# Softmax divisions ahead of the gated outputs, an output projection by tiles, and weight sums at period ends, in a one-core encoder kernel

## The chip, the cores and the metric

The kernel runs on one core of a Trainium2 chip. The metric is the device time of one execution in microseconds (us); smaller is better. The core has five engines that work side by side, each through its own queue in order: TensorE (PE, matmuls; its weight loads are shown apart as PEld), VectorE (DVE), ScalarE (ACT), GpSimd (POOL) and SyncE (SP, which issues DMAs).

## The reference

Two inputs, a prompt of 2048 tokens and a sample of 512, each of width 1024, go through the same two layers and a final RMSNorm. All is float32.

```python
# layer 0: windowed grouped-query attention, 16 heads of 64, 4 key/value heads
h = rmsnorm(x, g)
z = h @ w_in                                  # q, k, v, gate
scores = q . k * 64**-0.5 + bias              # |i-j| <= 128: blocks of 128 queries see 3 blocks of keys
m = max(max(scores), sink)
p = exp(scores - m)
p = p / (sum(p) + exp(sink - m))              # the division of this case
o = p @ v
x = x + (o * silu(gate)) @ w_out              # gated outputs, output projection
# layer 1: h = rmsnorm(x); f = Re(2-D DFT of h, per channel group)
x = x + (f * silu(h @ w_gate)) @ w_fout
y = rmsnorm(x, final_norm)
```

## The kernel before

Every large float32 product is made of three matmuls in a faster format: each operand is split into a high part and a low part (the rest), and hi·hi, hi·lo and lo·hi are summed (`matmul3`, L95). So most tiles exist as a high part, cast by ScalarE, and a low part, subtracted by VectorE or GpSimd.

**Stages.** The attention layer goes over five chunks of 512 tokens: chunk 0 is the sample, 1 to 4 the prompt. The Fourier layer follows. A chunk begins with h, k and v, and then has 17 *periods*, n = 0 to 16. Period n takes two blocks of 128 queries (b0 and b1) of one pair of heads (j = 0, 1; pair p = n // 2) through the first half of attention, and the two blocks of the period before ("old") through the second half:

- first half: `scores` (PE, L441, into three banks `spt`), `biased` (DVE, L460: adds the bias, finds the row's extreme), `exps` (ACT, L468, with the row's sum), `divide` (a reciprocal on DVE, L476, then a multiplication of the block by it: on ACT, L478, or on DVE, L480; in chunk 0 the form on DVE that also writes its accumulator, L484);
- second half, in the next period: `transp` (PE, L499: four banks `pt`), `parts` (hi by ACT, L507; lo by DVE, L508), `av` (PE, L525), `out_evac` (t2, a copy by ACT, L534; two sums o by DVE, L543, which free the bank; o times the gate on POOL, L545), and, one period later, `split` of the gated output uT (hi by ACT, L548; lo by POOL, L549).

PE's time between these is filled with pieces (`work`) of the next pair's q and gate projections, 8 pieces of three matmuls each, with `quota` saying how many pieces stand in each half of a period. When a projection is complete, its evacuation follows: `evac_q` (ACT L388, DVE L389, in chunk 0 after a scaling at L284) or `evac_g` (ACT L396, DVE L398). In the last periods there is no such work left, and pieces of the output projection (`op`, L95) take its place: uT times the weights wo, half of the 1024 columns at a time, four tiles of 128 tokens, in the three `spt` banks and one of five rotating banks; what remains of it (`tail`) is done before the next chunk's k and v.

**Extras** are steps for later stages, put at fixed quarters of a period: squares of the next chunk's tokens (ACT, L162), parts of sums of the Fourier layer's weights (`gate_sums`, `out_sums`: copies by ACT, L643 and L680, pieces by POOL, L624) and their stores. `AT` is the list of quarters of the weight sums.

**Order.** Each engine executes its queue in order. `seq` ties an instruction behind the one that was last tied on the same engine, and `after` ties it behind a named one; everything that is not tied a scheduler may move. A head pair's `start` loads its bias rows and copies two columns into them (DVE, L422 and L423). Times in the text are from the profiled execution, and a "+" in front of one counts from the start of a period's first scores.

Of the kernel before, what the change touches and what calls it, by code (L numbers as in the profile page):

```python
# [43 lines left out]
def encoder(  # L44
# [97 lines left out]
    def attention_phase():  # L142

        with ExitStack() as es:
# [265 lines left out]
            def attention(c, p, res, uTs):  # L410
# [61 lines left out]
                def divide(b, j):  # L472
# [3 lines left out]
                    seq(DVE, DVE.reciprocal(den, den))  # L476
                    if j:
                        seq(ACT, ACT.activation(s[:, ks], s[:, ks], AF.Copy, scale=den))  # L478
                    elif c:
                        seq(DVE, DVE.tensor_scalar(s[:, ks], s[:, ks], den, None, ALU.mult))  # L480
                    else:


                        seq(DVE, DVE.tensor_scalar(s[:, ks], s[:, ks], den, None, ALU.mult, ALU.add, accum_out=s[:, 386:387]))  # L484
# [74 lines left out]
            def out_proj(c, uTs):  # L559
# [3 lines left out]

                def mm(half, k):
                    if k == 0:

                        st["ps"] = (spt if half == 0 else []) + [bank(f"op{c}_{half}_{i}") for i in range(3 * (1 - half), 4)]
                    if k % 2 == 0:
                        st["w"] = load_w(c, 20 + half * 4 + k // 2, f"o{c}_{half}_{k}")
                    hi, lo = st["w"]  # L570
                    ws = slice((k % 2) * 512, (k % 2) * 512 + 512)
                    for i in range(4):
                        cs = slice(i * P, (i + 1) * P)
                        a = (uTs[k][0][:, cs], uTs[k][1][:, cs])
                        matmul3(st["ps"][i], a, (hi[:, ws], lo[:, ws]), k == 0, k == KD - 1)
# [34 lines left out]

                for half in range(2):
                    for k in range(KD):
                        steps.append(lambda half=half, k=k: mm(half, k))
                    steps.append(lambda half=half: evac(half))
                return steps
# [10 lines left out]
            def gate_sums(k):  # L626
# [10 lines left out]
                def lower():  # L637
                    b21 = rows[1][:, 0]
                    t = xtile([P, 2, 512], F32R, f"wB21_{k}")
                    after(ACT.copy(t[:, 0], b21), last_exp[0])  # L640
                    pieces(t[:, 1], b21, f32(t[:, 0]), ALU.subtract)
# [15 lines left out]
            def out_sums(k):  # L657
# [19 lines left out]
                def split(dst, row, half):  # L677
                    src = rows[row][:, half]
                    t = xtile([P, 2, 512], F32R, f"e{k}_{row}{half}")
                    after(ACT.copy(t[:, 0], src), last_exp[0])  # L680
                    pieces(t[:, 1], src, f32(t[:, 0]), ALU.subtract)
# [13 lines left out]
            stores = []  # L695
            AT = (1, 2, 5, 9, 11, 15, 16, 19, 23, 27, 28, 31, 32)
            EXTRA = {c: dict(zip(AT, gate_sums(c - 1) + out_sums(c - 1))) for c in range(1, 5)}
            for steps in EXTRA.values():
                steps.update({i: store for i in (4, 12, 18, 30, 34)})

# [41 lines left out]
            for c in range(len(CHUNKS)):  # L742
# [31 lines left out]
                m = 15 * KD - ahead_n  # L774
                quota = [m * (i + 1) // 27 - m * i // 27 for i in range(27)] + [3, 3, 2]
                assert sum(quota) == len(work) - ahead_n
# [20 lines left out]
                for n in range(17):  # L797
# [13 lines left out]
                    if new:  # L811
                        for j in range(2):
                            new[0].biased(new[1], j)
                        new[0].scores(new[1] + 1, (spt[2], spt[0]))
                    if old:
                        for b in range(2):
                            old[0].parts(old[1] + b)
                    if new:
                        for j in range(2):
                            new[0].exps(new[1], j)  # L820
                        for j in range(2):
                            new[0].biased(new[1] + 1, j)
                    for i in range(quota[2 * n] if n < 15 else 0):
                        work.pop(0)()
                    if n >= 15:
                        for i in range(n - 14):
                            op.pop(0)()
                    if new:
                        new[0].divide(new[1], 0)
                        for j in range(2):  # L830
                            new[0].exps(new[1] + 1, j)
                    if split:
                        split()
                        split = None
                    for i in range(4 * n, 4 * n + 2):
                        extra(i)
                    if old:
                        old[0].av(old[1])
                    if new:
                        new[0].divide(new[1], 1)  # L840
                        new[0].divide(new[1] + 1, 0)
                    if old:
                        split = old[0].out_evac(old[1])
                    if new:
                        new[0].divide(new[1] + 1, 1)
                    for i in range(4 * n + 2, 4 * n + 4):
                        extra(i)
                    if n < 15:
                        for i in range(quota[2 * n + 1]):
                            work.pop(0)()  # L850
                    elif n == 15:
                        op.pop(0)()
                    else:
                        split()
                        for i in range(3):
                            op.pop(0)()
                chain.pop(PE)
# [808 lines left out]
```

## Time and profile before

| what | value |
|---|---|
| time, three runs | 1708.18, 1713.01, 1712.97 us (median 1712.97) |
| profiled execution | 1707.01 us, span 1705.2 us, mean granted clock 0.983 |
| busy share of the span | PE 96%, PEld 79%, DVE 65%, ACT 54%, POOL 26% |
| attention layer's periods, chunks 0 to 4 | from about 42 us to 1128 us of the span |
| q1 (SP's DMA queue) | 81708 packets, 297.91 MB, 50.3% of 16 engines' span |

The span is the time from the first to the last instruction of the profiled execution; its own time, 1707.01 us, is 1.8 us more. "Busy" counts an engine's instructions, not its waits. PEclk or granted clock is the share of TensorE's full speed that the chip's throttle allowed. An arrow "<-" behind an instruction names what ended the engine's idle time before it. L numbers are lines of the kernel before.

### The profile page before, as it was taken

Reading aid. Unit: us, or ns where it says so; the run is one execution under the profiler, and the core shown is the slowest. Engines: PE = TensorE matmul, PEld = TensorE weight load, DVE = VectorE, ACT = ScalarE, POOL = GpSimd, SP = SyncE. Lnnn points to the kernel's source line nnn. Section 1 sums busy time; section 2 is a strip of 40 time slices with the busy share of each in tenths; the row PEclk is TensorE's granted clock in tenths of the full one; section 3 lists DMA queues with packets and bytes.
Section 4 is the critical chain, followed back from the end, with each engine's and each line's share of the span. In section 5 each row is a group of like instructions: output and inputs, shape, how many; then the busy total and the mean of one; then the engine's idle time right before and its main releaser. Section 6 shows DMA issues by size and latency. Waiting matters only on the chain.

```text
span 1705.2 us, 27749 instructions
## 1 busy us (share of the span) xinstructions
PE 1632.8 (96%) x9835; PEld 1348.5 (79%) x9835; DVE 1104.6 (65%) x2703; ACT 918.6 (54%) x2123; POOL 437.5 (26%) x605
## 2 busy tenths in 40 slices
PE   9888899999999998999999999989999999999998
PEld 7676688777797776887777877778888888888886
DVE  5766645676536665447764266656776667989686
ACT  6666633777516776247783176654545554443342
POOL 2344461332312421404223033121211111101010
PEclk9988999999999999999999999999999999999999
DMA  7467586756575564756556765566644568745862
GB/s 293 176 219 262 172 276 254 241 188 235 183 253 205 185 224 158 279 207 229 179 184 231 261 241 180 185 228 229 246 162 173 190 240 324 268 187 196 316 218 99
DMA packets 100646, 374.17 MB, mean 219 GB/s; under 512 B 12140, under 2 KB 22380, under 8 KB 83101
## 3 DMA queue, kind: packets, MB, share of 16 engines
q1 hardware_dynamic: 81708, 297.91, 50.3%
q0 software_dynamic: 16464, 70.30, 10.6%
q10 hardware_dynamic: 2336, 4.20, 0.7%
q8 instruction: 78, 1.28, 0.3%
q14 instruction: 60, 0.48, 0.1%
HBM read 281.10 MB, written 91.26 MB: 218 GB/s over the span
## 4 chain that ended last, share of the span: by engine, by line
PE 68%; ACT 9%; DVE 8%; DMA 8%; issue 4%; POOL 2%; SPq 0%; DVEq 0%; POOLq 0%; ACTq 0%
PE spt L95 8%; PE op L95 8%; PE qp L95 8%; PE gp L95 7%; PE fo L95 6%; PE W L95 6%; PE vp L95 3%; PE z L95 3%; PE spt L441 3%; ACT S L478 3%; PE Z L95 3%; PE Wo L95 2%; PE av L525 2%; DVE o L543 2%; PE pt L499 2%
## 5 line engine op out<-in xcount | busy, mean ns | idle before, releaser
L95 PE MATMUL gp<-h,wg 128*128 128x512 f32 x960 | 244.4, 403 | 0.0
L95 PE MATMUL qp<-h,wq 128*128 128x512 f32 x960 | 241.0, 401 | 0.0
L95 PEld LDWEIGHTS gp<-h,wg 128*128 128x128 f32 x960 | 178.4, 192 | 45.1 <-issue 10.3
L95 PEld LDWEIGHTS qp<-h,wq 128*128 128x128 f32 x960 | 178.2, 191 | 42.4 <-issue 5.2
L468 ACT ACTIVATE S<-S 128x385 f32<-128x385 f32 (+1 forms) x320 | 189.3, 602 | 22.5 <-DVE S L460 22.5
L508 DVE TENSOR_TENSOR pts<-pt,pts 128x384 fp32r<-128x384 f32 (+1 forms) x320 | 148.4, 523 | 41.0 <-ACT pts L507 40.8
L460 DVE CUSTOM_DVE_ANT_0 S<-spt,b 128x385 f32<-128x385 f32 (+1 forms) x320 | 156.1, 525 | 27.4 <-PE spt L441 26.9
L478 ACT ACTIVATE S<-S 128x384 f32<-128x384 f32 (+1 forms) x160 | 95.0, 595 | 102.8 <-DVE S L476 101.3
L549 POOL TENSOR_TENSOR uT<-o,uT 128x256 fp32r<-128x256 f32 x75 | 61.8, 823 | 328.2 <-ACT uT L548 328.1
L95 PE MATMUL op<-wo,uT 128*128 128x512 f32 x600 | 142.6, 389 | 0.0
L441 PE MATMUL spt<-kwin,qab 64*128 64x384 f32 (+1 forms) x960 | 129.4, 362 | 13.0 <-DVE S L460 9.9
L95 PE MATMUL fo<-wo,tTu 128*128 128x512 f32 x576 | 138.9, 392 | 0.0
L95 PEld LDWEIGHTS op<-wo,uT 128*128 128x128 f32 x600 | 112.7, 188 | 23.6
L507 ACT CAST pts<-pt 128x384 fp32r<-128x384 f32 (+1 forms) x320 | 124.4, 472 | 12.2 <-PE pt L499 10.3
L543 DVE TENSOR_TENSOR o<-av,t 64x256 f32<-64x256 f32 x150 | 62.6, 417 | 102.2 <-ACT t L534 94.3
L499 PE MATMUL pt<-ident,S 64*128 64x64 f32 x1792 | 89.4, 228 | 34.9 <-ACT S L478 19.5
L95 PEld LDWEIGHTS fo<-wo,tTu 128*128 128x128 f32 x576 | 106.0, 188 | 20.2
L525 PE MATMUL av<-pts,v 128*128 128x512 f32 (+1 forms) x576 | 118.7, 345 | 2.5 <-ACT pts L507 1.9
L525 PEld LDWEIGHTS av<-pts,v 128*128 128x128 f32 x576 | 101.0, 189 | 24.7 <-ACT pts L507 3.9
L441 PEld LDWEIGHTS spt<-kwin,qab 64*128 64x128 f32 x960 | 81.1, 189 | 45.1 <-issue 19.4
L499 PEld LDWEIGHTS pt<-ident,S 64*128 64x128 f32 x1792 | 76.9, 138 | 50.1 <-ACT S L478 29.2
L95 PE MATMUL spt<-wo,uT 128*128 128x512 f32 x360 | 97.4, 419 | 10.8 <-DVE S L460 10.8
(304 smaller groups left out, 2947.2 us busy)
## 6 DMA issues: line engine op xcount, KB each, us to landing
wo<-wsd SPq DMA_DIRECT2D x32, 1024.0 KB, 5.8
wq<-wsd SPq DMA_DIRECT2D x31, 1024.0 KB, 6.5
wg<-wsd SPq DMA_DIRECT2D x31, 1024.0 KB, 4.8
x<-x1d SPq DMA_DIRECT2D x40, 512.0 KB, 3.7
b<-b21d SPq DMA_DIRECT2D x40, 512.0 KB, 5.7
b<-rowd SPq DMA_DIRECT2D x40, 384.0 KB, 4.4
xs<-in_x_dram SPq DMA_DIRECT2D x23, 512.0 KB, 6.5
s2d<-gt POOLq DMA_DIRECT2D x40, 256.0 KB, 3.6
```

The source lines that it names most:

```text
L95: pe(PE.matmul(out, a[i], b[j], start=start and i + j == 0, stop=stop and i == 1, skip_group_check=more))
L441: pe(PE.matmul(banks[j][:, 2 + k0 * P : 2 + k1 * P], res["q"][rows, qp, b * P : (b + 1) * P], kwin[g][rows, kp, b * P + k0 * P : b * P + k ...
L460: seq(DVE, DVE.tensor_tensor_reduce(out=s[:, e0:e1], in0=ps[:, 1 + e0 : 1 + e1], in1=st["bias"][:, j, 386 - e1 : 386 - e0][:, ::-1], scale ...
L468: last_exp[0] = seq(ACT, ACT.activation(s[:, e0:e1], s[:, e0:e1], AF.Exp, bias=s[:, 386:387], scale=-1.0, accum_out=s[:, 387:388]))
L478: seq(ACT, ACT.activation(s[:, ks], s[:, ks], AF.Copy, scale=den))
L499: pe(PE.transpose(ps[h][:, kb, j, :], ss[j][rows, 1 + kb * P : 1 + (kb + 1) * P], ident[rows, rows]))
L507: seq(ACT, ACT.copy(hi, ps[:, k0:k1]))
L508: seq(DVE, DVE.tensor_tensor(lo, ps[:, k0:k1], f32(hi), ALU.subtract))
L525: pe(PE.matmul(to, v, pt, start=n == part == 0, stop=part == 1 and n in (1, len(todo) - 1), skip_group_check=n > 1,))
L543: seq(DVE, DVE.tensor_tensor(o[64 * j : 64 * j + 64], ps[0:64, :, j], t2[:, :, j], ALU.add))
L549: low = eng.tensor_tensor(lo, o, f32(hi), ALU.subtract)
```

## The change

Four things are edited. (1) In `divide`, one of four multiplications in a period stays on ScalarE (block b0, j = 1); the other three are on VectorE, where two were. (2) In a period, block b1's biased scores and exponentials and all four divisions are now issued ahead of the first half's projection pieces, av and `out_evac`; in period 15 both blocks' biased scores come ahead of `parts`. (3) All extras of a period stand at its end, `AT` and the stores' quarters are shifted, and ScalarE's copies of the weight sums are tied in its chain. (4) The output projection is issued by tiles: tile 3, in its bank, for k = 0 to 5, then tiles 0 to 2 for k = 0 to 5, then all tiles; its first four pieces stand in period 14. Periods 14, 15 and 16 hold 24, 33 and 39 matmuls of projections (before 15, 24 and 60), period 13 holds 24 (before 21).

```diff
-                    if j:
+                    if j > b % 2:
                         seq(ACT, ACT.activation(s[:, ks], s[:, ks], AF.Copy, scale=den))
                     elif c:
                         seq(DVE, DVE.tensor_scalar(s[:, ks], s[:, ks], den, None, ALU.mult))
...
-                def mm(half, k):
-                    if k == 0:
+                def mm(half, k, tiles):
+                    if k == 0 and 3 in tiles:
                         st["ps"] = (spt if half == 0 else []) + [bank(f"op{c}_{half}_{i}") for i in range(3 * (1 - half), 4)]
-                    if k % 2 == 0:
-                        st["w"] = load_w(c, 20 + half * 4 + k // 2, f"o{c}_{half}_{k}")
-                    hi, lo = st["w"]
+                    if k % 2 == 0 and 3 in tiles:
+                        st["w", k // 2] = load_w(c, 20 + half * 4 + k // 2, f"o{c}_{half}_{k}")
+                    hi, lo = st["w", k // 2]
...
-                    for i in range(4):
+                    for i in tiles:
...
-                for half in range(2):
-                    for k in range(KD):
-                        steps.append(lambda half=half, k=k: mm(half, k))
-                    steps.append(lambda half=half: evac(half))
+                steps += [lambda k=k: mm(0, k, (3,)) for k in range(6)]
+                steps += [lambda k=k: mm(0, k, range(3)) for k in range(6)]
+                steps += [lambda k=k: mm(0, k, range(4)) for k in range(6, KD)]
+                steps.append(lambda: evac(0))
+                steps += [lambda k=k: mm(1, k, range(4)) for k in range(KD)]
+                steps.append(lambda: evac(1))
...
-                    after(ACT.copy(t[:, 0], b21), last_exp[0])
+                    seq(ACT, ACT.copy(t[:, 0], b21))
...
-                    after(ACT.copy(t[:, 0], src), last_exp[0])
+                    seq(ACT, ACT.copy(t[:, 0], src))
...
-            AT = (1, 2, 5, 9, 11, 15, 16, 19, 23, 27, 28, 31, 32)
+            AT = (1, 4, 6, 9, 13, 17, 18, 20, 23, 26, 27, 32, 33)
...
-                steps.update({i: store for i in (4, 12, 18, 30, 34)})
+                steps.update({i: store for i in (7, 12, 22, 30, 37)})
...
-                quota = [m * (i + 1) // 27 - m * i // 27 for i in range(27)] + [3, 3, 2]
+                quota = [m * (i + 1) // 27 - m * i // 27 for i in range(27)] + [4, 4]
...
+                    if n == 15:
+                        for j in range(2):
+                            new[0].biased(new[1] + 1, j)
                     if old:
                         for b in range(2):
                             old[0].parts(old[1] + b)
                     if new:
                         for j in range(2):
                             new[0].exps(new[1], j)
-                        for j in range(2):
-                            new[0].biased(new[1] + 1, j)
-                    for i in range(quota[2 * n] if n < 15 else 0):
-                        work.pop(0)()
-                    if n >= 15:
-                        for i in range(n - 14):
-                            op.pop(0)()
-                    if new:
+                        if n < 15:
+                            for j in range(2):
+                                new[0].biased(new[1] + 1, j)
                         new[0].divide(new[1], 0)
                         for j in range(2):
                             new[0].exps(new[1] + 1, j)
+                        new[0].divide(new[1], 1)
+                        for j in range(2):
+                            new[0].divide(new[1] + 1, j)
+                    for i in range(quota[2 * n] if n < 15 else 18 - n):
+                        (work or op).pop(0)()
                     if split:
                         split()
                         split = None
-                    for i in range(4 * n, 4 * n + 2):
-                        extra(i)
                     if old:
                         old[0].av(old[1])
-                    if new:
-                        new[0].divide(new[1], 1)
-                        new[0].divide(new[1] + 1, 0)
-                    if old:
                         split = old[0].out_evac(old[1])
-                    if new:
-                        new[0].divide(new[1] + 1, 1)
-                    for i in range(4 * n + 2, 4 * n + 4):
+                    for i in range(4 * n, 4 * n + 4):
                         extra(i)
-                    if n < 15:
-                        for i in range(quota[2 * n + 1]):
-                            work.pop(0)()
-                    elif n == 15:
-                        op.pop(0)()
-                    else:
+                    if n == 16:
                         split()
-                        for i in range(3):
-                            op.pop(0)()
+                    half = quota[2 * n + 1] if n < 14 else 4 if n == 14 else 2
+                    for i in range(half):
+                        (work or op).pop(0)()
```

How the engines' queues change is shown at three places. Names carry chunk, pair, block and j: S2_5_0_1 is chunk 2, pair 5, block 0, j = 1; o, t2, av and pts name the old blocks' tiles; th and qab are the evacuations of a gate and of q; xs are the next chunk's tokens.

ScalarE in period 10 of chunk 2, before:

```order
L507 CAST pts2_4_2_6841<-pt2_4_3_1_6857 128x6x64
L468 ACTIVATE S2_5_0_0_6870<-S2_5_0_0_6870 128x385
L468 ACTIVATE S2_5_0_1_6872<-S2_5_0_1_6872 128x385
L396 ACTIVATE th2_5_6906<-gp2_5_6817 128x512
L468 ACTIVATE S2_5_1_0_6890<-S2_5_1_0_6890 128x385
L468 ACTIVATE S2_5_1_1_6892<-S2_5_1_1_6892 128x385
L548 CAST uT2_4_6335<-o2_4_0_6809 128x256
L162 ACTIVATE xs3_0_6815,ss3_6417<-xs3_0_6815 128x1024
L478 ACTIVATE S2_5_0_1_6872<-S2_5_0_1_6872 128x384
L534 COPY t22_4_2_6932<-av2_4_2_6919 64x512
L478 ACTIVATE S2_5_1_1_6892<-S2_5_1_1_6892 128x384
L507 CAST pts2_5_0_6966<-pt2_5_0_0_6967 128x6x64
```

and after:

```order
L507 CAST pts2_4_2_6841<-pt2_4_3_1_6857 128x6x64
L468 ACTIVATE S2_5_0_0_6870<-S2_5_0_0_6870 128x385
L468 ACTIVATE S2_5_0_1_6872<-S2_5_0_1_6872 128x385
L468 ACTIVATE S2_5_1_0_6890<-S2_5_1_0_6890 128x385
L468 ACTIVATE S2_5_1_1_6892<-S2_5_1_1_6892 128x385
L162 ACTIVATE xs3_0_6815,ss3_6438<-xs3_0_6815 128x1024
L478 ACTIVATE S2_5_0_1_6872<-S2_5_0_1_6872 128x384
L396 ACTIVATE th2_5_6916<-gp2_5_6817 128x512
L548 CAST uT2_4_6335<-o2_4_0_6809 128x256
L534 COPY t22_4_2_6931<-av2_4_2_6922 64x512
L162 ACTIVATE xs3_1_6938,ss3_6438<-xs3_1_6938 128x1024
L507 CAST pts2_5_0_6966<-pt2_5_0_0_6967 128x6x64
```

One division (L478) is left, ahead of the gate's evacuation (L396) and of t2 (L534); a square (L162) stands between t2 and the next period's casts (L507).

VectorE in the same period, before:

```order
L398 SCALAR_TENSOR_TENSOR s2_5_6908<-th2_5_6906,gp2_5_6817 128x512
L476 RECIPROCAL S2_5_0_0_6870<-S2_5_0_0_6870 128x1
L480 TENSOR_SCALAR S2_5_0_0_6870<-S2_5_0_0_6870 128x384
L476 RECIPROCAL S2_5_0_1_6872<-S2_5_0_1_6872 128x1
L476 RECIPROCAL S2_5_1_0_6890<-S2_5_1_0_6890 128x1
L480 TENSOR_SCALAR S2_5_1_0_6890<-S2_5_1_0_6890 128x384
L543 TENSOR_TENSOR o2_4_2_6934<-av2_4_2_6919,t22_4_2_6932 64x256 x2
L476 RECIPROCAL S2_5_1_1_6892<-S2_5_1_1_6892 128x1
L460 ISA S2_5_2_0_6995<-spt0_227,b2_5_6584 128x385
```

and after:

```order
L476 RECIPROCAL S2_5_0_0_6870<-S2_5_0_0_6870 128x1
L294 CAST kwin_230<-kwin_230 128x2x256
L480 TENSOR_SCALAR S2_5_0_0_6870<-S2_5_0_0_6870 128x384
L476 RECIPROCAL S2_5_0_1_6872<-S2_5_0_1_6872 128x1
L476 RECIPROCAL S2_5_1_0_6890<-S2_5_1_0_6890 128x1
L480 TENSOR_SCALAR S2_5_1_0_6890<-S2_5_1_0_6890 128x384
L476 RECIPROCAL S2_5_1_1_6892<-S2_5_1_1_6892 128x1
L480 TENSOR_SCALAR S2_5_1_1_6892<-S2_5_1_1_6892 128x384
L398 SCALAR_TENSOR_TENSOR s2_5_6918<-th2_5_6916,gp2_5_6817 128x512
L543 TENSOR_TENSOR o2_4_2_6933<-av2_4_2_6922,t22_4_2_6931 64x256 x2
L460 ISA S2_5_2_0_6995<-spt0_227,b2_5_6580 128x385
```

A third multiplication (L480) has come, and the last reciprocal no longer stands behind the sums o (L543); the gate's evacuation (L398) now stands behind the divisions. In chunk 0, where q is scaled first, the copy of two bias columns stands in this group after the change:

```order
L476 RECIPROCAL S0_1_2_1_920<-S0_1_2_1_920 128x1
L422 COPY b0_3_993<-sk_295 128x2
L423 COPY b0_3_993<-sk_295 128x2
L476 RECIPROCAL S0_1_3_0_938<-S0_1_3_0_938 128x1
L484 TENSOR_SCALAR S0_1_3_0_938<-S0_1_3_0_938 128x256
L476 RECIPROCAL S0_1_3_1_940<-S0_1_3_1_940 128x1
L484 TENSOR_SCALAR S0_1_3_1_940<-S0_1_3_1_940 128x256
L389 SCALAR_TENSOR_TENSOR qab0_2_956<-qp0_2_823,qab0_2_956 128x512
```

Before, L422 stood between the scaling of q (L284) and L389, ahead of all four divisions of the period; now L389 stands behind them.

TensorE in period 15 of chunk 2, before (the end of block b1's scores, then pieces of the projection):

```order
L441 MATMUL spt0_227<-kwin_230,qab2_7_7275 128x384
L95 MATMUL spt0_227<-wo2_0_0_7490,uT2_0_5586 128x512 x3
L95 MATMUL spt1_228<-wo2_0_0_7490,uT2_0_5586 128x512 x3
L95 MATMUL spt2_229<-wo2_0_0_7490,uT2_0_5586 128x512 x3
L95 MATMUL op2_0_3_7489<-wo2_0_0_7490,uT2_0_5586 128x512 x3
L525 MATMUL av2_7_0_7510<-pts2_7_0_7436,v1_4_3050 128x512 x2
```

and after:

```order
L441 MATMUL spt0_227<-kwin_230,qab2_7_7285 128x384
L95 MATMUL op2_0_3_7430<-wo2_0_4_7516,uT2_4_6335 128x512 x3
L95 MATMUL op2_0_3_7430<-wo2_0_4_7516,uT2_5_6584 128x512 x3
L95 MATMUL spt0_227<-wo2_0_0_7431,uT2_0_5586 128x512 x3
L95 MATMUL spt1_228<-wo2_0_0_7431,uT2_0_5586 128x512 x3
L95 MATMUL spt2_229<-wo2_0_0_7431,uT2_0_5586 128x512 x3
L525 MATMUL av2_7_0_7535<-pts2_7_0_7453,v1_4_3050 128x512 x2
```

Six matmuls of tile 3, in its own bank, now stand between the last scores and the first use of the score banks by the projection.

## The prediction

> **What bounds the kernel.** I read the page's engine shares first, then TensorE's waits, then windows by stage, then the timeline around one wait.
>
> ```profile
> span 1705.2 us, 27749 instructions
> ...
> PE 1632.8 (96%) x9835; PEld 1348.5 (79%) x9835; DVE 1104.6 (65%) x2703; ACT 918.6 (54%) x2123; POOL 437.5 (26%) x605
> ```
>
> TensorE (PE) is the bound: it idles only 1705.2 − 1632.8 = 72.4 us. The change adds no matmul and takes none away, so all it can win is this idle time and what the clock loses after it. TensorE's waits, longest sums first (total us, times, longest):
>
> ```profile
> PE pt L499 <- ACT S L478: 19.5, 52, 0.5
> PE pt L499 <- DVE o L543: 12.8, 16, 1.2
> PE spt L95 <- DVE S L460: 10.8, 5, 2.4
> PE spt L441 <- DVE S L460: 9.9, 10, 2.0
> PE spt L441 <- DVE qab L389: 3.1, 3, 1.7
> ```
>
> All five end at instructions that the change moves: the division on ScalarE (L478), the sums o that free a bank (L543), the biased scores (L460) and the low part of q (L389). They make 56.1 us. The third has five cases, one for each chunk.
>
> Windows by stage follow (start:end, length, then busy us and count for PE, PEld, DVE, ACT, POOL, then the granted clock). Rows 1, 3, 5, 7, 9 are periods 0 to 14 of the five chunks, rows 2, 4, 6, 8, 10 are period 15 up to the end of av. The last four are single periods: one without a wait and one with a stall in chunk 0, then the same for the prompt chunks.
>
> ```profile
> 42.20:201.50 159.30, 140.55 (x886) 108.72 (x885) 112.40 (x365) 109.54 (x274) 73.83 (x107) 0.93 0.59 209
> 201.50:213.10 11.60, 7.75 (x51) 6.20 (x51) 6.85 (x26) 6.61 (x17) 4.79 (x7) 0.85 0.53 173
> 292.80:432.90 140.10, 133.63 (x940) 106.32 (x939) 93.91 (x325) 101.53 (x265) 42.85 (x57) 1.00 0.61 207
> 432.90:445.00 12.10, 8.23 (x51) 6.39 (x51) 6.23 (x23) 5.87 (x16) 1.45 (x2) 0.86 0.56 184
> 519.70:664.30 144.60, 137.70 (x982) 109.44 (x981) 98.39 (x324) 105.53 (x265) 43.28 (x57) 1.00 0.58 200
> 664.30:677.20 12.90, 9.19 (x58) 7.12 (x58) 6.61 (x23) 6.04 (x16) 1.46 (x2) 0.74 0.51 173
> 751.80:893.30 141.50, 137.01 (x981) 109.20 (x980) 98.31 (x325) 104.36 (x262) 43.15 (x57) 1.00 0.57 199
> 893.30:906.00 12.70, 9.16 (x57) 7.15 (x57) 6.56 (x23) 6.04 (x16) 1.46 (x2) 0.73 0.52 177
> 974.70:1115.80 141.10, 135.52 (x937) 108.36 (x936) 95.18 (x318) 96.48 (x253) 41.83 (x57) 0.98 0.55 197
> 1115.80:1128.00 12.20, 8.15 (x57) 6.54 (x57) 6.07 (x21) 5.83 (x16) 1.47 (x2) 0.86 0.84 302
> 92.80:101.60 8.80, 8.80 (x65) 7.16 (x64) 7.30 (x14) 7.45 (x18) 7.38 (x12) 1.00 0.43 120
> 77.40:92.80 15.40, 12.21 (x65) 9.06 (x64) 10.76 (x37) 7.65 (x20) 6.15 (x10) 0.78 0.76 270
> 616.30:625.50 9.20, 9.20 (x69) 7.49 (x68) 6.23 (x21) 7.43 (x19) 1.68 (x2) 1.00 0.59 229
> 1019.00:1031.80 12.80, 11.15 (x71) 8.77 (x70) 7.90 (x26) 7.98 (x20) 7.78 (x11) 0.87 0.55 201
> ```
>
> First reading: idle is length less PE busy, 18.8, 6.5, 6.9, 4.5 and 5.6 us in the periods, 3.9, 3.9, 3.7, 3.5 and 4.1 at the ends: 61.4 of the 72.4. Second: a stall costs more than its idle time. The same 65 matmuls took 8.80 us and 15.40: 6.60 lost, 3.19 of it idle, the rest under a clock of 0.78. In the last pair 3.6 were lost, 1.65 idle. So about 2 us go for each idle us of a long stall.
>
> [...]
>
> **The pool to win.** I held the 14 periods 1 to 14 of each chunk against a no-wait period of their shape (8.80 to 9.2 us, less 0.24 for each matmul that a late period lacks); the excess sums to 32.3 us in chunk 0 and 7.9, 10.4, 7.3 and 8.5 in the others, 34.1 together. An end has 12 matmuls fewer than a full period, 9.20 − 12 × 0.24 = 6.3 us (5.9 for the two of x51): excess 5.7, 6.2, 6.6, 6.4, 5.9 = 30.8. All: 97.2 us. The profiled execution took 1707.01 us, its span and 1.8 beside it, 0.35% under the median of 1712.97; the floor is 1707.0 − 97.2 = 1609.8.
>
> **Divisions and order in the period.** One chain of chunk 2:
>
> ```profile
> 625.16 0.58 ACT L534 COPY t<-av 64x512 f32<-64x512 f32 x1
> ...
> 625.84 0.85 DVE L543 TENSOR_TENSOR o<-av,t 64x256 f32<-64x256 f32 x2 [1.85 <-ACT t L534]
> ...
> 626.98 0.62 ACT L478 ACTIVATE S<-S 128x384 f32<-128x384 f32 x1 [1.24 <-DVE S L476]
> ...
> 627.65 0.40 PE L499 MATMUL pt<-ident,S 64*128 64x64 f32 x6 [0.44 <-ACT S L478]
> ```
>
> The period's last division stands behind t2 and o, and the next period's transposes wait for it, 0.44 us here. After, all four divisions stand ahead of av. From the order and durations I schedule a period from its first scores: exponentials end at +5.6 us (block 1's scores are biased by +4.7), divisions at +7.0, t2 at +7.8, o at +8.7; the next transposes start at 9.2 + 0.7 = +9.9. So the first two waits have over 1 us of slack. ScalarE loses 80 × 0.62 us, one a period: 7.43 to 6.8 of 9.20. VectorE gains one of these (minimum/median/maximum ns):
>
> ```profile
> L480 DVE TENSOR_SCALAR S<-S x128: 349/423/834, 299.2 to 1123.0; 128x384 f32<-128x384 f32 x112, 128x256 f32<-128x256 f32 x16
> L484 DVE TENSOR_SCALAR_CACHE_REDUCE S<-S x32: 480/545/616, 46.8 to 208.7; 128x256 f32<-128x256 f32 x16, 128x384 f32<-128x384 f32 x16
> ```
>
> 64 of 0.42 in the prompt chunks, 16 of 0.55 with a short read in chunk 0: 6.23 to 6.7 of 9.20, so 2.5 us stay free, and I cost the 80 at nothing. If that cover went, they would cost 80 × 0.42 = 34. Prompt chunks: 34.1 falls to about 10, a gain of 24 (bounds: 5, below).
>
> **Chunk 0** is another matter:
>
> ```profile
> 74.20 2.82 POOL L119 TENSOR_TENSOR wq<-w32q,wq 128x256 fp32r<-128x256 f32 x4
> ...
> 74.65 3.55 DVE L422 COPY b<-sk 128x2 f32<-128x2 f32 x1
> ```
>
> The seven such copies of the chunk, grouped:
>
> ```profile
> L422 DVE COPY b<-sk 128x2 f32<-128x2 f32 x7 | 12.0, 1709 | 0.1
> ```
>
> A copy of 2 columns (L422) takes 3.55 us while POOL computes a weight's low parts, and everything on VectorE queues behind it. The stalled period of 15.40 follows directly. Three so held make 11.3 of the 12.0 us. Each precedes a stalled period (15.4, 14.2 and 15.8 us against 8.8): 19 of the 32.3. After, the copy stands among block 1's divisions, where POOL can hold it just as well; behind it now wait two divisions (1.4 us) and then q's low part (L389), which the next scores need. I take it that two of three recur at some 5 us and that the remaining 13 falls to 6: 16 stay, a gain of 16. Bounds: 4 left if none meets a string; 19 + 3 × 2 × 1.4 + 4 = 31 left if all do.
>
> [...]
>
> **Extras at the period's end.** Squares and copies for later weights now stand behind t2, and the next casts of p (L507) must follow them.
>
> ```profile
> 1015.03 0.62 ACT L680 CAST e<-w32e 128x512 fp32r<-128x512 f32 x1 [2.46 <-issue]
> L162 ACT ACTIVATE xs<-xs 128x1024 f32<-128x1024 f32 x23 | 24.4, 1062 | 2.8 <-DMA xs<-in_x_dram 2.5
> ```
>
> From +7.8, two copies end at +9.0, two squares at +10.3; the casts are wanted at +10.4. One that finds its buffer or its data late holds all of ScalarE, as at 1015.03, where the exponentials came 2.46 us late. Each extra's place behind its load stays or grows, so I leave 1.5 us a chunk, inside the 10 above. If each chunk had two waits of 2.5 us at 2 us per idle us, 4 × 10 = 40 would be lost, and the prompt chunks would gain nothing: that is the lower bound, −6. The upper is 34 − 5.
>
> **Last periods.** Now the projection's tiles 0 to 2 need the score banks, so they wait for block 1's biased scores:
>
> ```profile
> 671.23 4.03 PE L95 MATMUL spt<-wo,uT 128*128 128x512 f32 x9 [2.08 <-DVE S L460]
> ...
> 677.18 2.23 PE L95 MATMUL spt<-wo,uT 128*128 128x512 f32 x9
> ```
>
> 2.08 us of wait, then nine matmuls at 4.03 instead of 2.23. After, tile 3 in a bank of its own gives 12 matmuls in period 14 and 6 in period 15 ahead of these; the biased scores move ahead of the casts' low parts. By the schedule they end at +3.7, and tile 0 is reached at +2.7 + 1.4 = +4.1. Period 14 grows to a full one, so that its divisions are ready too. Low parts end at +5.7, av starts at +6.3. No wait for a weight's DMA is among TensorE's waits, so I cost their earlier use at nothing. Between the last t2 and the next chunk's k and v, 15 matmuls fewer (3.6 us) hide that chunk's preparation: I charge 1 us in all (bounds 0 and 3.6 for each of four handovers). 30.8 falls to 5, a gain of 26 (bounds 15 to 30).
>
> **Sum.** 24 + 16 + 26 = 66 less 1 for the handovers: 1707 − 65 = 1642.
>
> **Rivals.**
> 1. Only the idle time comes back, the clock stays as often low. For it: granted clocks return late after a stall (4.03 for nine). Against: the no-wait periods have 1.00 on both sides of stalls. Idle regained in proportion: 18.8 × 16/32.3 + 23.5 × 24/34.1 + 19.1 × 26/30.8 = 42, so 1665.
> 2. Chunk 0 keeps all (31 left) behind L422: 1707 − 50 = 1657. For it: the copy's place and POOL's strings are both still there; against: in most periods they miss one another (7 copies, 3 held).
> 3. ScalarE blocked by extras that wait for DMA ahead of the casts: the 24 is lost, 1666. For it the 2.46 above; against, only two such waits in four chunks stalled TensorE long.
> 4. The waits only change their name: L389's q or the banks become late by as much as the divisions were; then 1707 ± 5. Against: the 2.5 us free on VectorE.
> 5. Slower: VectorE becomes the bound through L480 held by POOL. It decides from 2.5 us of hold-up per period; at 3.4, the size of L422's hold, in all 64 prompt periods at 2 us per idle us, 64 × 0.9 × 2 = 115, less the ends' 26: about 1796; in a third of them and with the other gains lost, about 1720. Against: L480's maximum in 128 is 0.83.
>
> **Chances.** Forecast 0.60 (own range 1620 to 1655), rivals 1 to 5: 0.08, 0.13, 0.10, 0.04, 0.05. Of these only the fourth lies within 0.3% (5 us, about what measurement can tell) and only the fifth is slower: faster 0.91, same 0.04, slower 0.05. Range: from most of the floor's pool, 1620, to rivals 1 and 3 with a little over, 1672.
>
> **What would show it.** The first two waits should nearly vanish, the third fall under 2 us in all, ends be 7 to 8 us long at a clock near 1, periods 0 to 14, which now hold 12 matmuls (2.9 us) more, 135 to 141 us in the prompt chunks and about 146 in chunk 0; L422 should still show two or three rows over 3 us. L478 should read x80, L480 x192. I am wrong if ScalarE's L507 waits for extras, if L389 leads TensorE's waits in the prompt chunks, or if windows shrink only by their idle time.

## The result, and the profile after

The changed kernel takes 1619.82 us (median of 4 runs, 1618.31 to 1622.40) against 1711.74 us before (4 runs): the ratio is 0.9468, with a 95% interval of 0.9448 to 0.9488, so 92 us less. The forecast was 1642; the time lies 22 us under it, at the lower edge of its range of 1620 to 1672. The profiled execution after took 1622.40 us with a span of 1620.6, the longest of its runs, while that of before (1707.01) lay under all of its own; between the two profiles 84.6 us of span are gone, and the readings below go by these.

The page of the changed kernel, engine shares:

```profile
span 1620.6 us, 27520 instructions
## 1 busy us (share of the span) xinstructions
PE 1598.9 (99%) x9835; PEld 1334.6 (82%) x9835; DVE 1116.6 (69%) x2799; ACT 870.2 (54%) x2043; POOL 431.1 (27%) x605
```

The same 9835 matmuls: TensorE's idle time fell from 72.4 to 21.7 us, and its busy time from 1632.8 to 1598.9. So 50.7 us of the gain were waits, and 33.9 are less busy time for the same matmuls.

Its waits, the five longest sums:

```profile
PE spt L441 <- DVE S L460: 5.6, 7, 2.0
PE As L95 <- ACT gs L1190: 2.3, 1, 2.3
PE pt L499 <- ACT xs L162: 1.2, 2, 0.8
PE idle L227 <- DVE idle L224: 1.2, 1, 1.2
PE spt L95 <- ACT h L205: 1.2, 1, 1.2
```

The wait for ScalarE's division (19.5 us before) is gone from the list, that for o is 0.4 us in all, and the five waits of the chunks' ends are gone. What is left of L460 is mostly each chunk's period 0, which the change doesn't touch.

The windows by stage: periods 0 to 14 of the five chunks, each followed by period 15 up to the end of av (columns as in the prediction). Periods 0 to 14 now hold 12 matmuls (2.9 us) more, the ends 3 (0.7 us) more.

```profile
42.16:178.98 136.82, 132.86 (x898) 105.91 (x898) 112.45 (x399) 103.29 (x262) 75.95 (x110) 0.98 0.67 244
178.98:185.65 6.67, 6.67 (x55) 5.67 (x54) 5.34 (x24) 4.50 (x14) 2.54 (x5) 1.00 0.79 273
261.91:396.27 134.36, 133.58 (x952) 107.64 (x951) 99.26 (x343) 93.39 (x252) 41.89 (x58) 1.00 0.62 223
396.27:403.10 6.83, 6.83 (x54) 5.73 (x54) 5.26 (x21) 4.71 (x14) 0.46 (x1) 1.00 0.33 90
474.39:612.58 138.19, 137.32 (x994) 111.69 (x994) 103.13 (x343) 97.36 (x252) 41.93 (x58) 1.00 0.60 217
612.58:619.65 7.07, 7.07 (x61) 6.02 (x60) 5.53 (x21) 4.92 (x14) 0.40 (x1) 1.00 0.33 91
690.88:830.01 139.13, 137.35 (x994) 111.55 (x994) 102.99 (x343) 96.05 (x249) 41.81 (x58) 1.00 0.59 210
830.01:837.09 7.08, 7.08 (x60) 6.01 (x60) 5.53 (x21) 4.93 (x14) 0.40 (x1) 1.00 0.38 91
902.34:1036.68 134.34, 133.85 (x947) 108.41 (x947) 97.26 (x336) 88.10 (x240) 41.30 (x58) 1.00 0.59 214
1036.68:1043.57 6.89, 6.89 (x60) 5.97 (x60) 5.09 (x19) 4.72 (x14) 0.64 (x1) 1.00 1.03 384
```

The ends are without a wait, at a full clock. Length before less length after plus the added matmuls gives the gains by stage: chunk 0's periods 159.30 − 136.82 + 2.9 = 25.4 us; the prompt chunks' 8.6 + 9.3 + 5.3 + 9.7 = 32.9; the ends 5.6 + 6.0 + 6.5 + 6.3 + 6.0 = 30.4; together 88.7. The first instruction of the Fourier layer on TensorE moved from 1171.0 to 1083.2 us, 87.8 earlier, so 0.9 was given back between the chunks. The other 3.2 us were lost inside the Fourier layer, which the change doesn't touch: one wait there took 2.3 us instead of 0.6, and behind it the granted clock was 0.50 for 3.4 us (1362.87 to 1366.28).

A chain of the changed kernel in period 5 of chunk 2:

```profile
524.67 0.60 ACT L478 ACTIVATE S<-S 128x384 f32<-128x384 f32 x1
524.94 0.15 DVE L476 RECIPROCAL S<-S 128x1 f32<-128x1 f32 x1
525.13 0.42 DVE L480 TENSOR_SCALAR S<-S 128x384 f32<-128x384 f32 x1
526.07 0.58 ACT L534 COPY t<-av 64x512 f32<-64x512 f32 x1
526.76 0.85 DVE L543 TENSOR_TENSOR o<-av,t 64x256 f32<-64x256 f32 x2 [0.28 <-ACT t L534]
```

The period began at 519.16. The last division ends at 525.55, +6.4, ahead of t2; the sums o end at +8.5, and the first weight load of the next transposes starts at 528.84, 3.3 us after the division.

### The profile page after: what moved, and what is told of

It is laid out like the page before. It is cut to its first block, busy times and chain, and to the rows that moved or that the text cites. A ratio compares the mean times of both kernels' runs of the same rounds, so it can differ in the third digit from the quotient of the medians.

```text
span 1620.6 us, 27520 instructions
## 1 busy us (share of the span) xinstructions
PE 1598.9 (99%) x9835; PEld 1334.6 (82%) x9835; DVE 1116.6 (69%) x2799; ACT 870.2 (54%) x2043; POOL 431.1 (27%) x605
## 4 chain that ended last, share of the span: by engine, by line
PE 87%; DMA 5%; DVE 4%; ACT 2%; issue 1%; POOL 1%; SPq 0%; POOLq 0%; DVEq 0%; ACTq 0%
PE qp L95 13%; PE gp L95 12%; PE op L95 8%; PE spt L95 8%; PE W L95 6%; PE spt L441 6%; PE av L525 6%; PE fo L95 5%; PE z L95 4%; PE vp L95 4%; PE Z L95 3%; PE pt L499 3%; PE Wo L95 2%; PE X L95 2%; PE trb L940 1%; DMA xs<-in_x_dram 1%
## 5 line engine op out<-in xcount | busy, mean ns | idle before, releaser
L95 PE MATMUL gp<-h,wg 128*128 128x512 f32 x960 | 237.7, 396 | 0.0
L460 DVE CUSTOM_DVE_ANT_0 S<-spt,b 128x385 f32<-128x385 f32 (+1 forms) x320 | 156.9, 527 | 115.6 <-PE spt L441 115.2
L507 ACT CAST pts<-pt 128x384 fp32r<-128x384 f32 (+1 forms) x320 | 123.8, 472 | 185.6 <-PE pt L499 185.4
L549 POOL TENSOR_TENSOR uT<-o,uT 128x256 fp32r<-128x256 f32 x75 | 55.5, 740 | 358.9 <-ACT uT L548 358.9
L441 PEld LDWEIGHTS spt<-kwin,qab 64*128 64x128 f32 x960 | 85.1, 185 | 37.5 <-issue 27.5
L95 PE MATMUL spt<-wo,uT 128*128 128x512 f32 x360 | 86.7, 392 | 0.0
L480 DVE TENSOR_SCALAR S<-S 128x384 f32<-128x384 f32 (+1 forms) x192 | 79.2, 413 | 5.3
L543 DVE TENSOR_TENSOR o<-av,t 64x256 f32<-64x256 f32 x150 | 62.6, 417 | 26.4 <-ACT t L534 25.0
L95 PEld LDWEIGHTS spt<-wo,uT 128*128 128x128 f32 x360 | 66.5, 188 | 13.7
L499 PEld LDWEIGHTS pt<-ident,S 64*128 64x128 f32 x1792 | 68.8, 138 | 6.2 <-issue 2.3
```

The costliest lines, as they stand in the source:

```text
L95: pe(PE.matmul(out, a[i], b[j], start=start and i + j == 0, stop=stop and i == 1, skip_group_check=more))
L441: pe(PE.matmul(banks[j][:, 2 + k0 * P : 2 + k1 * P], res["q"][rows, qp, b * P : (b + 1) * P], kwin[g][rows, kp, b * P + k0 * P : b * P + k ...
L460: seq(DVE, DVE.tensor_tensor_reduce(out=s[:, e0:e1], in0=ps[:, 1 + e0 : 1 + e1], in1=st["bias"][:, j, 386 - e1 : 386 - e0][:, ::-1], scale ...
L499: pe(PE.transpose(ps[h][:, kb, j, :], ss[j][rows, 1 + kb * P : 1 + (kb + 1) * P], ident[rows, rows]))
L507: seq(ACT, ACT.copy(hi, ps[:, k0:k1]))
L543: seq(DVE, DVE.tensor_tensor(o[64 * j : 64 * j + 64], ps[0:64, :, j], t2[:, :, j], ALU.add))
```

## The experiments

Each ratio is to the kernel before, with its 95% interval. "Chunk" lengths are from one chunk's first scores to the next's (the last: to the Fourier layer), read from the trace of each run; before they were 250.6, 226.9, 232.1, 222.9 and 196.3 us, after 219.8, 212.5, 216.5, 211.5 and 180.8.

**The division rule alone.**

```diff
-                    if j:
+                    if j > b % 2:
```

> The kernel before with the division rule alone (one of four on ScalarE), old order. Theory A (the order is what matters: the last division stands behind t2 and the sums o): the chain keeps its length but for a VectorE division of 0.42 us in place of a ScalarE one of 0.62 and its hand-over of about 0.1; of the 19.5 us of waits for L478 some 12 go, the 12.8 us for o (L543) stay: 10 to 22 us faster, about 1695 us. Theory B (the divisions on ScalarE and their hand-over are what matters): most of the gain of the periods, 45 us or more, at most 1667 us.

Measured: 1711.17 us, 0.9989 (0.9975 to 1.0004): no difference, less than either theory gave. Chunk 0 took 242.9 us (7.7 less), the prompt chunks 1 to 3 us more each. TensorE's first wait has only changed its name, and the timeline of a prompt period shows why:

```profile
PE pt L499 <- DVE S L480: 16.7, 37, 0.6
```

```profile
622.91 0.73 POOL L545 TENSOR_TENSOR o<-o,s 128x256 f32<-128x256 f32 x1 [2.18 <-DVE o L543]
...
623.06 0.79 DVE L480 TENSOR_SCALAR S<-S 128x384 f32<-128x384 f32 x1
...
623.91 0.40 PE L499 MATMUL pt<-ident,S 64*128 64x64 f32 x6 [0.56 <-DVE S L480]
```

Behind o, the last division starts just after GpSimd has begun the product of o, and takes 0.79 us instead of 0.42; 59 of 192 such divisions took over 0.6 us. What VectorE saved against ScalarE's 0.62 it lost by standing in that place. The rule pays only with the order, as the next runs show.

**The order alone** (block b1's exponentials and the four divisions moved ahead of the projection pieces; division rule, extras and projection as before).

```diff
+                        new[0].divide(new[1], 0)
+                        for j in range(2):
+                            new[0].exps(new[1] + 1, j)
+                        new[0].divide(new[1], 1)
+                        for j in range(2):
+                            new[0].divide(new[1] + 1, j)
...
-                    if new:
-                        new[0].divide(new[1], 0)
-                        for j in range(2):
-                            new[0].exps(new[1] + 1, j)
...
                     if old:
                         old[0].av(old[1])
-                    if new:
-                        new[0].divide(new[1], 1)
-                        new[0].divide(new[1] + 1, 0)
                         split = old[0].out_evac(old[1])
-                    if new:
-                        new[0].divide(new[1] + 1, 1)
```

> The kernel before with the new order within a period alone: both blocks' biased scores, exponentials and all four divisions ahead of the projection pieces, av and the sums; division rule, extras and output projection as before. Theory A: the waits for L478 and L543 nearly vanish, the ends of the chunks stay: 45 to 62 us faster, about 1657 us. Theory B: with two divisions of 0.62 us left on ScalarE, no more than 20 us faster, 1692 us or more.

Measured: 1658.67 us, 0.9686 (0.9665 to 0.9707), 53 us less, as theory A had it, and against theory B: this gain comes with two divisions still on ScalarE. The waits then:

```profile
PE spt L95 <- DVE S L460: 11.8, 5, 2.5
PE spt L441 <- DVE S L460: 10.0, 12, 2.6
PE pt L499 <- DVE o L543: 5.4, 11, 1.0
```

The five ends are all still there, and the wait for L478 is gone from the list.

**Rule and order together.**

> Division rule and new order together, extras and output projection as before. Theory A: within 6 us of the order alone, about 1653 us. Theory B: the gain is the sum of both, and the division rule gives at least 25 us over the order alone.

Measured: 1645.21 us, 0.9596 (0.9580 to 0.9612): 13.5 us under the order alone. Theory A's 6 us were too few, theory B's 25 too many. The chunks took 223.8, 216.9, 221.7, 216.1 and 185.5 us against 232.1, 218.4, 224.4, 219.8 and 185.9 for the order alone: 8.3 of the 16.6 lie in chunk 0, where ScalarE also casts the weights, and 8.3 in the prompt chunks. (The profiles differ by 13.9 in span; the rest was lost after the chunks.)

**The projection by tiles alone.**

> The kernel before with the output projection by tiles alone (with its quotas and the biased scores of period 15 ahead of the casts). If the ends are a matter of their own, as the prediction's sum has it: the five waits of about 2.1 us for L460 go and 20 to 30 us with them, about 1686 us. Rival: the ends are late because the divisions of period 14 are, and the wait only moves to the scores or the transposes: under 10 us faster, 1702 us or more.

Measured: 1675.59 us, 0.9777 (0.9761 to 0.9793), 36.5 us less, more than the 30.8 of the ends (between the two profiles 31.8). Its longest waits are the old ones of the periods:

```profile
PE pt L499 <- ACT S L478: 15.2, 40, 0.4
PE pt L499 <- DVE o L543: 12.6, 17, 1.2
```

From period 15 to the next chunk it took 7.3, 8.7, 9.1, 9.0 and 8.6 us less, 42.7, of which the 12 matmuls moved into earlier periods are 5 × 2.85 = 14.2; these earlier periods grew by only 10.4, so 3.9 more came from fuller last periods.

**The changed kernel with the old projection.**

> The changed kernel with the output projection and the quotas of the last periods as before. If the ends add up with the rest: the five waits of about 2 us come back with their slow clock, 25 to 31 us slower, about 1648. Rival: with the divisions early the ends would have been mended anyhow, under 10 us slower.

Measured: 1643.85 us, 0.9607 (0.9588 to 0.9626): 24 us slower than the changed kernel. So the projection by tiles is worth 36.5 alone and 24 on top of the rest; the parts are not additive. From period 15 on, this kernel already takes 0.3 to 1.8 us less a chunk than before (6.6 in all); rule and order together take 6.8 less there, the order alone 1.4, and what of them does it was not taken apart. That and the 3.9 above make 10.5 of the 12.5.

**The changed kernel with the old extras.**

> The changed kernel with the extras as before: two quarters ahead of av and two behind the sums, the old lists of quarters, the copies not tied in ScalarE's chain. If the extras' place matters as little as the prediction's sum took it: within 4 us of the changed kernel, 1616 to 1624. Rival (copies that wait for a store or stand between the casts cost long stalls, as at 1015.03 in the kernel before): 6 to 15 us slower, 1626 to 1635.

Measured: 1620.28 us, 0.9466 (0.9449 to 0.9483): no difference. Where the extras stand, and whether their copies are tied, is worth nothing that shows.

**The changed kernel with the old division rule.**

> The changed kernel with two of four divisions on ScalarE again. Theory A (order): the divisions still end over 1 us ahead of the transposes, within 4 us of the changed kernel. Theory B (ScalarE's load): ScalarE goes from about 6.8 to 7.4 of 9.2 us, squares and casts come late, 15 us slower or more.

Measured: 1626.26 us, 0.9507 (0.9485 to 0.9529), 6.4 us slower. All of it is chunk 0: 226.2 us against 219.8, the others 213.0, 216.4, 211.3 and 180.9 as in the changed kernel. Three waits for q's evacuation on ScalarE (L388), 3.7 us together, have come there. In this kernel ScalarE's load matters only in chunk 0; with the old extras and projection, where the rule was worth 8.3 us in the prompt chunks too, it mattered there as well.

**The held copy, in the kernel before.** The two columns of bias are multiplied by 1 in the form that writes its accumulator, and so is the second copy (L423):

```diff
-                DVE.tensor_copy(bt[:, :, 0], sk[:, 2 * p : 2 * p + 2])
+                DVE.tensor_scalar(bt[:, :, 0], sk[:, 2 * p : 2 * p + 2], 1.0, None, ALU.mult, ALU.add, accum_out=junk[:, 0:1])
```

> The kernel before; only the copies of two bias columns (L422 and the one behind it) become a multiplication by 1 in the form that also writes its accumulator, as chunk 0's divisions have it. If the copy was held by GpSimd's string and so caused chunk 0's three long stalls (15.4, 14.2, 15.8 us against 8.8): no such instruction over 0.4 us, those periods fall to 9 or 10 us, 12 to 19 us faster, about 1696 us. If the copy was only a bystander of a stall with another cause: within 4 us.

Measured: 1700.44 us, 0.9928 (0.9907 to 0.9948), 11.6 us less. The instruction (now at L423 of that kernel):

```profile
L423 DVE TENSOR_SCALAR_CACHE_REDUCE b<-sk x40: 150/157/158, 16.0 to 1079.7; 128x2 f32<-128x2 f32 x40
```

Never over 0.16 us, though it still falls into GpSimd's strings (at 74.57 us, 0.15 long, in one of four from 74.11 to 76.94), and the three stalled periods fell from 15.4, 14.2 and 15.8 us to 10.4, 9.7 and 11.3: the copy was the cause of 14.0 of the 19.0 us that they had over 8.8. Chunk 0 as a whole took 9.5 us less, since other periods of it grew.

**The held copy, in the changed kernel.**

> The changed kernel with the copies of two bias columns in the form that writes its accumulator. The changed kernel's trace still has three held copies in chunk 0, of 1.30 to 1.69 us. If the order has made room for them: the holds go and the time stays within 2 us, 1618 to 1622. Rival (they still cost, as the prediction's 16 us left in chunk 0 had it): 4 us faster or more.

Measured: 1620.96 us, 0.9468 (0.9448 to 0.9488): no difference. In the changed kernel's run the copies were still held, but not for long; the timeline and the two groups (minimum/median/maximum ns):

```profile
73.68 2.82 POOL L119 TENSOR_TENSOR wq<-w32q,wq 128x256 fp32r<-128x256 f32 x4
...
75.09 1.44 DVE L422 COPY b<-sk 128x2 f32<-128x2 f32 x1
```

```profile
L422 DVE COPY b<-sk x40: 146/169/1686, 16.3 to 1005.0; 128x2 f32<-128x2 f32 x40
```

```profile
L480 DVE TENSOR_SCALAR S<-S x192: 341/422/427, 264.9 to 1042.5; 128x384 f32<-128x384 f32 x168, 128x256 f32<-128x256 f32 x24
```

The copy got through when GpSimd's string of four ended, 1.4 us after it began, and there was slack for that. The divisions hardly met a GpSimd instruction: 4 of 192 overlapped one (58 of 128 before), with 64 more of them and a maximum of 427 ns where it was 834.

**Squares further behind their loads** (the changed kernel; in chunk 0 one square a period instead of two).

```diff
-                    if i:
-                        sq = ACT.activation(xs[i - 1], xs[i - 1], AF.Square, accum_out=ss[:, i - 1 : i])
+                    if i > 1:
+                        sq = ACT.activation(xs[i - 2], xs[i - 2], AF.Square, accum_out=ss[:, i - 2 : i - 1])
...
-                        if i >= (38 if c else 24) and i % 2 == 0 and norm_steps:
+                        if i >= (38 if c else 24) and i % (2 if c else 4) == 0 and norm_steps:
```

> The changed kernel with the squares of the next chunk's tokens one step further behind their loads, and in chunk 0 one for each period instead of two. What is left of the periods' excess lies where ScalarE's squares wait for their data or come in pairs (chunk 0, periods 8 and 9: 1.4 and 3.2 us; prompt chunk 3, period 12: 1.6). If that is their cause: 3 to 6 us faster than the changed kernel, about 1615. Rival: the stalls move to other extras or the loads come later: within 2 us.

Measured: 1620.69 us, 0.9467 (0.9449 to 0.9485): no difference in time, but a shift. Their cause was there; the changed kernel in prompt chunk 3, period 12:

```profile
801.40 1.06 ACT L162 ACTIVATE xs<-xs 128x1024 f32<-128x1024 f32 x1 [1.81 <-DMA xs<-in_x_dram]
...
802.59 0.17 DVE L88 TENSOR_SCALAR inv<-ss 128x4 f32<-128x4 f32 x1 [2.04 <-ACT xs L162]
...
803.33 0.79 PE L441 MATMUL spt<-kwin,qab 64*128 64x384 f32 x5 [1.29 <-DVE S L460]
```

A square waits for its tokens, the norm (L88) waits on VectorE for the square, and the biased scores behind it hold TensorE. With more distance this went: chunks 1 to 3 took 0.6, 0.5 and 1.7 us less. Chunk 0 gave 2.9 back, through the copy:

```profile
145.62 2.96 DVE L422 COPY b<-sk 128x2 f32<-128x2 f32 x1
145.73 2.81 POOL L119 TENSOR_TENSOR wg<-w32g,wg 128x256 fp32r<-128x256 f32 x4
...
151.46 0.50 PE L441 MATMUL spt<-kwin,qab 64*128 64x256 f32 x4 [2.58 <-ACT qab L388]
```

Shifted by a little, the copy met a string's start, was held for the whole of it, and q came 2.58 us late (a square of 1.04 us, moved by this edit, also stood ahead of q on ScalarE). So the 1.4 us of the changed kernel are luck of the meeting, not a mended cause.

**Twelve pieces ahead in chunk 0** (as the last; `ahead_n` 12 instead of 16).

> As the run of the squares; besides, chunk 0 begins its periods with 12 projection pieces done instead of 16, as the other chunks do, so that the first scores don't meet a gate's evacuation on VectorE. If the 2.0 us wait in chunk 0's period 0 and the slow clock behind it come from that evacuation: 2 to 4 us less than that run, about 1612. Rival: the weights of the second pair are not there yet, or the other chunks' 0.4 us is a floor of another kind: no gain or a loss of up to 5 us.

Measured: 1622.01 us, 0.9476 (0.9458 to 0.9493). Period 0's wait fell from 2.02 to 0.35 us, but a copy held for 3.10 us came with a wait of 2.53 us for q: nothing gained.

**Both small mendings** (squares further behind for the prompt chunks only, copies in the accumulator form).

> The changed kernel with the squares one step further behind their loads for the later prompt chunks only (chunk 0's own squares as in the changed kernel), and the copies of bias columns in the accumulator form. The run of the squares took 0.6, 0.5 and 1.7 us off chunks 1, 2 and 3 and gave 2.9 back in chunk 0; the run of the copies took 0.6 off chunk 0. If these add up: 3.4 us faster than the changed kernel in the profile, about 1617, at the edge of what can be told. Rival: the run-to-run spread hides it, 1620.

Measured: 1618.00 us, 0.9454 (0.9440 to 0.9467); chunks 217.6, 211.8, 216.1, 209.8 and 180.9. In the trace 4.9 us of the chunks are gone, 2.2 of them in chunk 0; the times hardly tell it from the changed kernel, whose interval overlaps.

## Why the prediction was right, and where it was mis-sized

*The mechanism.* The first two waits vanished, the third went with the ends, and L478 and L480 read x80 and x192, as foretold. The windows came out at or under the foretold lengths: 134.3 to 139.1 us in the prompt chunks, 136.8 in chunk 0, ends of 6.7 to 7.1. One sign failed: no L422 is over 3 us, the longest is 1.69. And not all five waits ended at something that the change moves: of the fourth, 5.6 of 9.9 us are left, mostly in the chunks' period 0. That the order does it, and not ScalarE's load, is shown by the order alone (53 us) beside the rule alone (nothing). The sum's cost of nothing for 80 divisions on VectorE held: no L480 took over 0.43 us and no L484 over 0.62, and they stand where they hardly meet GpSimd.

*A stall costs more than its idle time.* Rival 1, only the idle time comes back, fell: 50.7 us of idle time brought 84.6 us of span. The slow clock, which the prediction named, is only part of the other 33.9. The mean granted clock was 0.983 over 1705.2 us and then 0.995 over 1620.6, which is 29.0 and 8.1 us of full speed lost: 21 us at most. And in periods 0 to 14 of chunks 1 to 3 the clock reads 1.00 in both kernels, yet 23.2 us came back there for 14.4 us of idle time. Two periods of chunk 2 before, without a wait and with the one of 0.44 us, show what else is lost:

```profile
616.88 0.91 PE L499 MATMUL pt<-ident,S 64*128 64x64 f32 x24
617.60 0.88 PE L441 MATMUL spt<-kwin,qab 64*128 64x384 f32 x6
...
626.13 1.08 PE L499 MATMUL pt<-ident,S 64*128 64x64 f32 x18
627.65 0.40 PE L499 MATMUL pt<-ident,S 64*128 64x64 f32 x6 [0.44 <-ACT S L478]
627.86 0.77 PE L441 MATMUL spt<-kwin,qab 64*128 64x384 f32 x6
```

The scores behind the transposes start 0.72 us after the first of them, and then 1.73: 1.0 us is lost where the list has 0.44. The transposes overlap (24 of them, of 0.22 us each, take 0.91), and around the wait they do so less: 18 take 1.08 and the other six 0.40, while the list counts only the time in which none runs. All transposes together were busy for 89.4 us before and 70.4 after.

In the attention layer before, the granted clock fell to 0.50 eleven times, for 3.4 or 6.8 us each, while no single wait was over 2.4 us by the list.

*The terms.* The sum was 24 + 16 + 26 − 1; measured were 32.9, 25.4, 30.4 and −0.9. All three gains were sized too low, that is, too much was left:

- Prompt periods: 10 us left, measured about 1 (34.1 − 32.9). The 1.5 us a chunk for extras that hold ScalarE was too much: by the run of the squares they cost 0.6, 0.5 and 1.7 us in chunks 1 to 3 and nothing in chunk 4, and rival 3 has no more than that. (These 2.8 are more than the 1.2 left, so the pool of 34.1 was itself a little too small.)
- Chunk 0: 16 us left, measured 32.3 − 25.4 = 7. "Two of three recur at some 5 us" is the step that failed. Three copies were held again, but for 1.30 to 1.69 us instead of 3.55 to 4.20, and freeing them gained nothing (1620.96 us). What is left is mostly in periods 0, 8 and 9 of the chunk (10.0, 10.2 and 12.1 us, the first by 1.5 us of slow clock alone). The bounds (4 to 31) held it, and the run of the squares shows that the larger value was possible: a copy held for 2.96 us cost a wait of 2.58. So rival 2 is real but did not come.
- Ends: 5 left, measured 0.4. The schedule (bank reached at +4.1, biased scores done at +3.7) was tight and held: in chunk 2 it was +3.7 and +3.2, without a wait.
- Handovers: 1 charged, 0.9 measured.

The terms' errors add to 22.8 us; less the 3.2 lost in the Fourier layer that is the 19.6 by which the profiled execution (1622.40) lies under 1642.

*What was not foreseen.* The parts overlap: alone they give 53 (order), 36.5 (projection) and about 1 (rule, within the noise), and 92 together is near their sum only by accident, since the rule is worth 13.5 behind the order and the projection 12.5 less.

*VectorE beside GpSimd.* The hold-up that rival 5 feared was there in the old order: in the run of the division rule alone a division that met GpSimd's product of o took 0.79 us for 0.42, and 59 of 192 took over 0.6; in the changed kernel, with the new order, none took over 0.43. The copy of two bias columns took up to 4.20 us in the kernel before, and in the form that writes its accumulator 0.16 at most.

What stays open: in the Fourier layer of the profiled execution a cast on ScalarE (L1418) waited 2.40 us for a weight's DMA ahead of the late one (L1190; both lines of the changed kernel); why that DMA was late was not followed; other executions of the changed kernel had spans 2.0 to 4.1 us shorter.

## What to carry to other kernels

An instruction that the critical engine's next step needs should be queued ahead of everything that only the step after needs, even on an engine with idle time: here the place of four divisions and the two exponentials ahead of them was worth 53 us, the engine that the divisions run on nothing by itself. When a window is sized from TensorE's waits, an estimate from these two kernels is 1.7 times the idle time (84.6/50.7); look at its busy time for equal matmuls to see the rest: here a wait of 0.44 us cost 1.0 at a full clock. Before moving a step to VectorE, look in the timeline at what GpSimd starts at that place: behind o a division took 0.79 us instead of 0.42.

## What the hardware showed that was not expected

A VectorE copy of two columns that met an unbroken string of GpSimd's instructions was held until the string ended, not only one of them: it took 1.44 us from the middle of a string of 2.82, 2.96 at the start of one of 2.81, and up to 4.20 in the kernel before, where more instructions followed without a gap, against a median of 0.17:

```profile
L422 DVE COPY b<-sk x40: 157/169/4201, 16.2 to 1085.9; 128x2 f32<-128x2 f32 x40
```

Where GpSimd issued a DMA right behind the string, the hold lasted through that too. The copy of 3.55 us before ran from 74.65 to 78.20; a string of five products ended at 77.71, and the issue behind it at 78.24 (the two other held copies of that kernel ended the same way):

```profile
74.20 2.82 POOL L119 TENSOR_TENSOR wq<-w32q,wq 128x256 fp32r<-128x256 f32 x4
76.99 0.72 POOL L119 TENSOR_TENSOR wg<-w32g,wg 128x256 fp32r<-128x256 f32 x1
77.67 0.57 POOL L123 DMA_DIRECT2D wsd<-wq  x1
```

And TensorE's granted clock was 0.50 for 3.42 us behind two waits of 0.80 and 0.51 us in one period, and stayed at 1.00 behind a wait of 2.02 us in another. Period 9 in chunk 0 of the changed kernel, and the part of it at the low clock (columns as above):

```profile
123.09:135.15 12.06, 10.74 (x64) 8.45 (x64) 10.22 (x31) 10.23 (x23) 10.21 (x14) 0.86 0.70 255
127.24:130.66 3.42, 3.42 (x9) 2.69 (x9) 2.58 (x10) 3.42 (x9) 3.10 (x5) 0.50 0.19 78
```

With these two waits, 1.3 us of idle time in all, it ran at a granted 0.86 and took 3.3 us more than a period of its shape without a wait (8.8). Period 0 of chunk 0 has the same matmuls and the same single wait of 2.02 us in both kernels; here it is before and after:

```profile
42.20:50.72 8.52, 6.50 (x35) 4.87 (x34) 4.52 (x18) 4.97 (x12) 3.36 (x5) 1.00 0.60 247
42.16:52.21 10.05, 8.03 (x35) 5.89 (x35) 5.14 (x20) 4.35 (x11) 3.34 (x5) 0.83 0.50 209
```

The clock stayed at 1.00 in one and fell in the other, which cost 1.5 us. What decides this, no run here shows.
